# Nine up-projection pairs of a float32 encoder layer by seven half-size products

## The chip, the core and the metric

One core of a Trainium2 chip runs the whole layer in one launch. The metric is the device time of one execution in microseconds (us). The engines are named as the profile names them: PE (TensorE, matrix products), PEld (its weight loads), DVE (VectorE), ACT (ScalarE), POOL (GpSimd), SP (SyncE, which only issues DMAs here). SBUF is the on-chip memory of 128 partitions; PSUM holds the sums that PE writes, in banks of 128x512 float32. [...] A change of 0.2% of the time, 2.1 us, is about what a measurement of this kernel can tell from no change.

## What is computed

The last sub-layer, the gated MLP, is what the change touches (512 tokens, 1024 channels, 2816 hidden channels):

```python
hf = _rms_norm(x, norm_ffn_pre[l])
u = _dwconv_causal(hf @ w_up[l], ffn_dw[l]) + ffn_dw_b[l]
u_g, u_v = jnp.split(u, 2, axis=-1)
yff = (jax.nn.silu(u_g) * u_v) @ w_down[l]
x = x + _rms_norm(yff, norm_ffn_post[l])
```

`w_up` holds the 2816 gate columns and then the 2816 value columns. The convolution has width 3 and runs along the tokens.

## The kernel before

Every float32 product is made of three: an operand is split into a rounded high part and the rest, and `mm3` (lines 253 to 257 before the change) issues high x high, high x low and low x high. A weight block comes from HBM into a raw tile; ACT casts it to the high part `wh` (line 201) and DVE subtracts to get the low part `wl` (line 202). `run_blocks` walks a list of jobs (a load, then a body of products) and prepares three jobs ahead; four `wh`/`wl` tiles go round, so a cast waits until PE is done with the block four splits earlier. A scheduler then sets the order of the instructions on each engine when the program is built; each engine works its list in that order, and an instruction that waits holds back all that stands behind it.

**Up projection** (`up_jobs`). The 22 gate/value pairs j are blocks of 128 columns: one gate job and one value job each, of 24 products of 128x512 (8 channel tiles, three products each), the activations `hth`/`htl` as the moving operand. The first four jobs (j = 0, 1) run in two token halves, as 128x256 products, since the second half of the tokens is normalized last. `done` evacuates a bank: ACT applies the last tap and the bias (line 1639), DVE adds the two other taps (line 624), and after the value block ACT takes silu and DVE multiplies into a quarter tile `qa`/`qb` (line 1645).

**Down projection.** It already uses Strassen's seven products over pairs of hidden tiles and column and token halves. Its weight sums are made during the up projection by `Sums`: two rows of blocks of `w_down` come in over ACT's DMA queue into `dw` tiles (line 568), four sums are made in place by DVE (lines 572 to 575), and the result is stored to DRAM over ACT's queue (line 579) and read back later by SP. Its activation sums are made by GpSimd from the quarter tiles (`activation_sums`, lines 596 to 599), four operations of 128x256 a pair. There are four `dw` tiles, and two row pairs are in flight.

Of the kernel before, what the change touches and what calls it, by code (L numbers as in the profile page):

```python
# [17 lines left out]
F32 = mybir.dt.float32  # L18
F32R = mybir.dt.float32r
AF = mybir.ActivationFunctionType  # L20
ALU = mybir.AluOpType
# [4 lines left out]
P = 128  # L26
# [60 lines left out]
def hybrid_layer(ctx: ExitStack, tc: tile.TileContext, a: dict, out: bass.AP):  # L87
# [120 lines left out]
    def cols(w, c0, n=P, k0=0, nk=NK):  # L208

        return w[k0 * P:(k0 + nk) * P, c0:c0 + n].rearrange("(k p) c -> p k c", p=P), [P, nk, n]  # L210
# [29 lines left out]
            body(*w)  # L240
            bg.tick()

    def matmul(ps, lhs, rhs, start, stop):
        steps_of[:] = [PE.matmul(ps, lhs, rhs, start=start, stop=stop).ins]  # L244
        bg.clock += max(int(math.prod(rhs.shape[1:])), 256) * 0.00042

    turns = []
# [2 lines left out]
        turns.append(PE.transpose(ps, x, ident[:n, :n]).ins)  # L250
        bg.clock += 0.107

    def mm3(ps, w_hi, w_lo, x_hi, x_lo, first, last):

        matmul(ps, w_hi, x_hi, first, False)
        matmul(ps, w_hi, x_lo, False, False)
        matmul(ps, w_lo, x_hi, False, last)

    def channel_major(ps, w, act, sl=slice(0, S), turn=None):

# [296 lines left out]
    class Sums:  # L557
# [9 lines left out]
                for i, x in enumerate(self.held[q]):  # L567
                    self.queue.dma_start(x, self.w[(2 * q + i) * P:(2 * q + i + 1) * P, :])

        def add(self, q):  # L570
            (b11, b12), (b21, b22) = ((x[:, :S], x[:, S:]) for x in self.held[q])
            V.tensor_tensor(b22, b22, b12, ALU.subtract)
            V.tensor_tensor(b12, b12, b11, ALU.subtract)
            V.tensor_tensor(b11, b22, b11, ALU.add)
            V.tensor_tensor(b21, b21, b11, ALU.subtract)

        def store(self, q):
            for i, x in enumerate(self.held.pop(q)):
# [15 lines left out]
    def activation_sums(x, z, eng):  # L594

        eng.tensor_tensor(x[:, 2], x[:, 1], z[:, 1], ALU.add)
        eng.tensor_tensor(x[:, 3], x[:, 0], x[:, 1], ALU.subtract)
        eng.tensor_tensor(x[:, 1], x[:, 2], x[:, 0], ALU.subtract)
        eng.tensor_tensor(z[:, 2], z[:, 0], x[:, 1], ALU.subtract)
# [597 lines left out]
    def then(f):  # L1197

        return None, None, f
# [420 lines left out]
    def open_ffn():  # L1620
        bg.drain("n1")
        close(ns.work_)
        close(ns.xp_)
        close(ns.xm_)
        ns.fp_, ns.fp = new_pool("ffn", False)
        ns.work = ns.fp
        ns.quart = [(ns.fp.tile([P, 4, S // 2], F32, tag=f"qa{q}", name="qa"),
                     ns.fp.tile([P, 3, S // 2], F32, tag=f"qb{q}", name="qb")) for q in range(NF // 2)]
        ns.post = ns.fp.tile([P, D], F32, name="g_ffn")
        G.dma_start(ns.post, a["norm_ffn_post"][0].partition_broadcast(P))  # L1630

    def up_jobs():
        st, held = {}, []

        def done(j, i, ps):
            if i == 0:
                st[j] = ns.fp.tile([P, 2, S], F32, tag="c", name="c", bufs=2)
            c, ch = st[j], i * NF + j
            st["first"] = A.activation(c[:, i], ps, AF.Identity, bias=pc("fb", ch), scale=pc("fdw2", ch)).ins
            st["taps"] = taps(c[:, i], ps, lambda k: pc("fdw01", k * 44 + ch), 3).ins  # L1640
            if i == 1:
                th = ns.fp.tile([P, S], F32, tag="th", name="th")
                A.activation(th, c[:, 0], AF.Silu)  # L1643
                x = ns.quart[j // 2]
                V.tensor_tensor(x[j % 2][:, 0:2].rearrange("p a b -> p (a b)"), th, c[:, 1], ALU.mult)
                if j % 2:
                    activation_sums(*x, G)


        for n in range(2 * NF):  # L1650
            def body(hi, lo, n=n):
                j, i = divmod(n, 2)
                if n > 3:
                    ps = bank()
                    channel_major(ps, (hi, lo), ns.hf)
                    done(j, i, ps)

                    q = n // 3 - 2
                    if 0 <= q < NF // 2:
                        with tc.issue_after(st["taps" if n % 3 == 0 else "first"]):  # L1660
                            (ns.sums.add, ns.sums.store, ns.sums.load)[n % 3](q + 2 * (n % 3 == 2))
                    return
                if n == 0:
                    bg.drain("n0")
                ps = bank(("mm", "sc")[n % 2])
                if n == 3:
                    channel_major(ps, (hi, lo), ns.hf, slice(0, S // 2), lambda: bg.drain("n1"))
                else:
                    (channel_major if n else by_pass)(ps, (hi, lo), ns.hf, slice(0, S // 2))
                held.append((j, i, ps, (hi, lo)))  # L1670
                if n == 3:
                    open_ffn()
                    for j, i, ps, w in held:
                        (channel_major if i or j else by_pass)(ps, w, ns.hf, slice(S // 2, S))
                        done(j, i, ps)
# [3 lines left out]
                    ns.sums.load(1)  # L1679
            yield *cols(w_up, n % 2 * DFF + n // 2 * P), body, V, same, HALF_SHIFT if n < 4 else 0  # L1680

    def down_jobs():
        pairs, hold, half = NF // 2, 4, S
# [7 lines left out]
                load_parts(raw, ns.sums.parts(phase, job, q))  # L1691
                raws.append(raw)

        def split_to(hi, lo, x):
            A.copy(hi, x)  # L1695
            V.tensor_tensor(lo, x, hi.bitcast(F32), ALU.subtract)  # L1696

        def activations(phase, q):

            if (phase, q) == (0, 0):  # L1700
                hi, lo = (gp.tile([P, WB], F32R, tag="wr", name="wr", bufs=2) for _ in range(2))
            elif (phase, q) == (1, pairs - 1):
                hi, lo = (ns.fp.tile([P, D], F32R, tag=f"qa{i}", name="a3") for i in range(2))
            else:
                if "slots" not in parts:
                    parts["slots"] = [t[:, i * 4:i * 4 + 4].rearrange("p a b -> p (a b)") for t in new_ht()
                                      for i in range(2)]
                slot = parts["slots"][(phase * pairs + q - 1) % 4]
# [3 lines left out]
            split_to(hi, lo, ns.quart[q][phase].rearrange("p a b -> p (a b)"))  # L1712
# [22 lines left out]

        def step(name, t, q, a, w, phase, cut=slice(0, S), ps=None):
            hi, lo = parts[phase, q]
            sl = slice(t * P, (t + 1) * P)
# [166 lines left out]
```

## Time and profile before

| | |
|---|---|
| time, median of 3 runs | 1040.89 us (1040.86 to 1042.05) |
| span of the profiled execution | 1039.2 us; its own time is not given apart from the span |
| PE busy | 1029.6 us, 99% |
| DVE / ACT / POOL busy | 819.5 / 510.9 / 153.2 us |
| up projection from the third pair on | from about 709 to 932 us of the span |
| down projection | from there to the end |

A row of a group reads: line, engine, operation, output and inputs, shape, count, then total busy time and mean of one, then the idle time of the engine ahead of it and what ended it. A row of one source line gives least, median and greatest duration in ns. A matmul's own duration overlaps its neighbours', so the pace of PE is read from the distance of starts.

### The profile page before, as it was taken

How to read it: one execution, taken by the hardware profiler on the slowest of the kernel's cores; microseconds unless marked ns; L12 is line 12 of the kernel's file. 1: busy time of each engine (PE TensorE's matmuls, PEld its weight loads, DVE VectorE, ACT ScalarE, POOL GpSimd, SP SyncE). 2: the span in 40 equal slices, each digit the busy share in tenths (PEclk: the TensorE clock that was granted, in tenths of full speed). 3: DMA queues.
4: the chain of work that ended last, by engine and by line, in shares of the span. 5: the costliest groups of instructions: out<-in, count | busy, mean ns of one | idle time of the engine just before them, and what ended most of it. 6: DMA issues, size and time to landing. Idle time of an engine off the chain costs nothing.

```text
span 1039.2 us, 14390 instructions
## 1 busy us (share of the span) xinstructions
PE 1029.6 (99%) x5189; PEld 876.3 (84%) x5189; DVE 819.5 (79%) x1263; ACT 510.9 (49%) x838; POOL 153.2 (15%) x235
## 2 busy tenths in 40 slices
PE   9999999999999999999999999999999999999997
PEld 8888888888888988888888899898888888888886
DVE  7999999577788668878687898767777767667796
ACT  5322222376565465765634566645333433445672
POOL 4001000100020214342000021121112121111002
PEclk9999999999999999999999999999999999999999
DMA  8954333334534345766467744145677676625662
GB/s 272 320 155 97 102 102 102 83 100 114 150 99 131 88 131 167 203 172 168 143 199 251 239 137 123 46 138 166 199 239 235 211 236 207 213 82 191 216 212 82
DMA packets 194125, 169.36 MB, mean 163 GB/s; under 512 B 25295, under 2 KB 165692, under 8 KB 194053
## 3 DMA queue, kind: packets, MB, share of 16 engines
q1 hardware_dynamic: 185011, 136.69, 43.9%
q10 hardware_dynamic: 6482, 23.21, 6.1%
q0 software_dynamic: 2560, 8.54, 2.8%
q8 instruction: 41, 0.67, 0.3%
q14 instruction: 31, 0.25, 0.1%
HBM read 142.18 MB, written 26.23 MB: 162 GB/s over the span
## 4 chain that ended last, share of the span: by engine, by line
PE 96%; DMA 2%; DVE 1%; ACT 0%; issue 0%; SPq 0%; POOL 0%; POOLq 0%; DVEq 0%; ACTq 0%
PE ps_mm L244 46%; PE ps_av L244 30%; PE ps_tr L244 11%; PE ps_sc L244 7%; PE ps_tr L250 1%; DMA turned<-e 1%; DMA ptl<-turned 1%; PE ps_mm L462 1%; PE ps_av L462 1%; DMA xs<-in_x 0%; DVE e L857 0%; DVE e L939 0%; DVE e L930 0%; PE ps_tr L446 0%; DVE wl L202 0%
## 5 line engine op out<-in xcount | busy, mean ns | idle before, releaser
L201 ACT CAST wh<-wr 128x1024 fp32r<-128x1024 f32 (+1 forms) x140 | 146.3, 1047 | 235.3 <-PE ps_mm L244 119.3
L202 DVE TENSOR_TENSOR wl<-wr,wh 128x1024 fp32r<-128x1024 f32 (+1 forms) x140 | 175.1, 1251 | 83.1 <-ACT wh L201 81.2
L244 PE MATMUL ps_mm<-hth,wh 128*128 128x512 f32 (+1 forms) x536 | 198.3, 377 | 0.0
L244 PE MATMUL ps_mm<-htl,wh 128*128 128x512 f32 (+1 forms) x536 | 198.3, 377 | 0.0
L244 PE MATMUL ps_mm<-hth,wl 128*128 128x512 f32 (+1 forms) x536 | 198.1, 377 | 0.0
L244 PE MATMUL ps_av<-htl,wh 128*128 128x512 f32 (+1 forms) x328 | 122.5, 373 | 0.0
L244 PE MATMUL ps_av<-hth,wh 128*128 128x512 f32 (+1 forms) x328 | 122.4, 373 | 0.0
L244 PE MATMUL ps_av<-hth,wl 128*128 128x512 f32 (+1 forms) x328 | 122.3, 373 | 0.0
L244 PEld LDWEIGHTS ps_mm<-hth,wh 128*128 128x128 f32 x536 | 99.1, 188 | 18.3 <-ACT hth L164 0.3
L244 PEld LDWEIGHTS ps_mm<-hth,wl 128*128 128x128 f32 x536 | 98.9, 188 | 18.2
L244 PEld LDWEIGHTS ps_mm<-htl,wh 128*128 128x128 f32 x536 | 99.0, 188 | 18.0
L697 DVE SCALAR_TENSOR_TENSOR y<-y,par,y 128x508 f32<-128x508 f32 (+29 forms) x120 | 82.8, 731 | 0.1
L244 PEld LDWEIGHTS ps_av<-hth,wl 128*128 128x128 f32 x328 | 61.7, 188 | 11.0
L244 PEld LDWEIGHTS ps_av<-htl,wh 128*128 128x128 f32 x328 | 61.5, 188 | 10.9
L244 PEld LDWEIGHTS ps_av<-hth,wh 128*128 128x128 f32 x328 | 61.6, 188 | 10.8
L1696 DVE TENSOR_TENSOR wl<-dw,wh 128x1024 fp32r<-128x1024 f32 x32 | 40.2, 1261 | 16.8 <-ACT wh L1695 16.6
L1695 ACT CAST wh<-dw 128x1024 fp32r<-128x1024 f32 x32 | 33.5, 1052 | 24.5 <-PE ps_tr L244 10.1
L1643 ACT ACTIVATE th<-c 128x512 f32<-128x512 f32 x22 | 13.9, 632 | 48.6 <-DVE c L624 48.6
L624 DVE SCALAR_TENSOR_TENSOR c<-ps_mm,par,c 128x510 f32<-128x510 f32 (+1 forms) x44 | 32.7, 744 | 0.7
L857 DVE STREAM_TRANSPOSE e<-e 128x128 f32<-128x128 f32 (+3 forms) x46 | 32.5, 729 | 0.2
L876 DVE TENSOR_TENSOR ptl<-ptl,pth 128x384 fp32r<-128x384 f32 (+3 forms) x42 | 20.7, 511 | 14.9 <-ACT pth L875 14.8
L244 PE MATMUL ps_tr<-htl,wh 128*128 128x512 f32 x80 | 31.7, 396 | 0.0
(518 smaller groups left out, 2238.5 us busy)
## 6 DMA issues: line engine op xcount, KB each, us to landing
wr<-in_w_up SPq DMA_DIRECT2D x44, 512.0 KB
wr<-in_w_in SPq DMA_DIRECT2D x38, 512.0 KB
wr<-in_w_gate SPq DMA_DIRECT2D x32, 512.0 KB
wp<-in_w_down ACTq DMA_DIRECT2D x22, 512.0 KB
sums<-wp ACTq DMA_DIRECT2D x22, 512.0 KB
dw<-sums SPq DMA_DIRECT2D x44, 256.0 KB
wr<-in_w_branch SPq DMA_DIRECT2D x16, 512.0 KB
wide<-in_w_out SPq DMA_DIRECT2D x12, 512.0 KB
```

Source lines behind the costliest of these rows:

```text
L201: last_weights[:] = [order(A.copy(hi, raw[:, :n])).ins, low.tensor_tensor(lo, raw[:, :n], hi.bitcast(F32), ALU.subtract).ins]
L202: low.tensor_tensor(lo, raw[:, :n], hi.bitcast(F32), ALU.subtract).ins]
L244: steps_of[:] = [PE.matmul(ps, lhs, rhs, start=start, stop=stop).ins]
L250: turns.append(PE.transpose(ps, x, ident[:n, :n]).ins)
L462: keep(PE.matmul(banks[c][:, :S // 2], w[p == 1][:, k, c * P:(c + 1) * P], ht[p == 2][:, i * 4 + k, :S // 2], start=(i, p, k) == (0, 0, 0) ...
L624: ins = V.scalar_tensor_tensor(dst[:, s:], src[:, :S - s], w(k), dst[:, s:], ALU.mult, ALU.add)
L697: ins = V.scalar_tensor_tensor(dst[:, s:], src[:, :S - s], pc("conv_dw", k * 4 + j), dst[:, s:], ALU.mult, ALU.add)
L857: V.transpose(dst, src.rearrange("p (t j b) -> p b t j", b=4, j=32))
L876: V.tensor_tensor(lo, raw, hi.bitcast(F32), ALU.subtract)
L1643: A.activation(th, c[:, 0], AF.Silu)
L1695: A.copy(hi, x)
L1696: V.tensor_tensor(lo, x, hi.bitcast(F32), ALU.subtract)
```

## The change

Pairs j = 3, 5, ... 19 get the seven products; each is followed by an ordinary pair j+1, and I call the two a group, 1 to 9. Pairs 0, 1, 2 and 21 stay ordinary. For a seven-product pair the two blocks are cut in halves by channels (a11, a12 the gate block, a21, a22 the value block), and the activations in halves by channels and tokens. Each product then has 4 channel tiles, three products each, of 128x256: 7 x 12 = 84 products of 128x256 where there were 48 of 128x512.

- `token_sums`: once, GpSimd makes four sums of activations (eight operations of 128x1024, lines 1639 and 1641), and ACT and DVE split them into `tokh`/`tokl` (lines 1646, 1647).
- For each seven-product pair both blocks come into two `dw` tiles (named `wq`, line 1740), and GpSimd makes four sums of 128x512 in place and in `sums2` (lines 1732 to 1735). Four splits follow: the gate block (for step a), s2 and s1 (step b), the changed value block (step c) and half of the gate tile (step d, 128x512). The products run as a (24), b (24), c (12), d (12) and e (12, with the weights of c).
- Banks: the results gather in one `sc` and one `tr` bank; three 128x256 copies by ACT (lines 1757, 1763, 1765) and three 128x256 additions by DVE in PSUM (lines 1759, 1770, 1774) stand between the products.
- The `w_down` row sums of pairs 1 to 10 go from DVE to GpSimd (`add`, four operations of 128x512 a group); pair 0 stays on DVE. One pair is loaded ahead, not two.
- The value block of the ordinary pair is cut in two halves of 12 products around c and d.
- The activation sums of the down projection are three operations (lines 1658 to 1660), made from the last group on, and a fourth (line 1862) after the split of phase 0; the split of a pair in phase 0 is two of 128x512, not one of 128x1024.

```diff
-        def add(self, q):
+        def add(self, q, eng=V):
...
-            V.tensor_tensor(b22, b22, b12, ALU.subtract)
+            eng.tensor_tensor(b22, b22, b12, ALU.subtract)
...
+    def token_sums():
...
+        for i, (k, t) in enumerate(((0, 0), (1, 1), (0, 1), (1, 0))):
+            x = [h.bitcast(F32)[:, 4 * k:4 * k + 4, cut[t]] for h in ns.hf]
+            G.tensor_tensor(raw[i], *x, ALU.add)
+        for out, a, b in ((0, 2, 0), (2, 1, 2), (1, 1, 0), (3, 3, 1)):
+            G.tensor_tensor(raw[out], raw[a], raw[b], ALU.subtract)
+        for i in (1, 0, 2, 3):
+            split_to(hi[:, i], lo[:, i], raw[i])
...
+    def down_sums(*pairs):
+
+        for q in pairs:
+            x, t = ns.quart[q], ns.pair_sums[q]
+            G.tensor_tensor(t[:, 0], x[:, 1], x[:, 3], ALU.add)
+            G.tensor_tensor(t[:, 1], x[:, 0], x[:, 1], ALU.subtract)
+            G.tensor_tensor(x[:, 1], t[:, 0], x[:, 0], ALU.subtract)
...
+            def load_a():
+                z.g, z.v = [load_block(j, i) for i in range(2)]
+                w = split_weights(z.g, [P, NK, P], shift=HALF_SHIFT)
+                z.s = ns.fp.tile([P, D], F32, tag="z7", name="sums2")
...
+                G.tensor_tensor(s1, a21, a22, ALU.add)
+                G.tensor_tensor(s2, s1, a11, ALU.subtract)
+                G.tensor_tensor(a21, a11, a21, ALU.subtract)
+                G.tensor_tensor(a12, a12, s2, ALU.subtract)
...
+            def load_block(j, i):
+                raw = ns.fp.tile([P, D], F32, tag="dw", name="wq", bufs=4)
...
+            yield a
+            yield then(lambda q=q: ns.sums.load(q + 1))
+            yield plain(j + 1, 0)
+            yield b
+            yield then(lambda q=q: ns.sums.add(q + 1, G))
+            yield (*block(j + 1, 1), first_half)
...
+            yield c
+            yield d
+            yield then(lambda q=q: ns.sums.store(q + 1))
+            yield then(lambda j=j, f=second_half: f(j + 1))
+            yield e
```

**GpSimd's list**, in the middle of the up projection. Before, the activation sums of two pairs (`qa`, `qb` are quarter tiles):

```order
L597 TENSOR_TENSOR qa_6866<-qa_6866 128x256 [waits DVE_49]
L596 TENSOR_TENSOR qa_6866<-qa_6866,qb_6867 128x256 [waits DVE_49]
L598 TENSOR_TENSOR qa_6866<-qa_6866 128x256 [waits Pool_49]
L599 TENSOR_TENSOR qb_6867<-qb_6867,qa_6866 128x256 [waits Pool_49]
L597 TENSOR_TENSOR qa_6868<-qa_6868 128x256 [waits DVE_49]
```

Now, one whole group, the sixth (`wq_8041` and `wq_8043` are its gate and value blocks, `wp_8180` and `wp_8181` two rows of `w_down`):

```order
L1732 TENSOR_TENSOR sums2_8049<-wq_8043 128x512 [waits DMAHW2_49,DVE_49]
L1733 TENSOR_TENSOR sums2_8049<-sums2_8049,wq_8041 128x512 [waits DMAHW1_49,Pool_49]
L1734 TENSOR_TENSOR wq_8043<-wq_8041,wq_8043 128x512 [waits DMAHW6_49]
L572 TENSOR_TENSOR wp_8181<-wp_8181,wp_8180 128x512 [waits DMAHW4_49,DMAHW3_49,DVE_49]
L1735 TENSOR_TENSOR wq_8041<-wq_8041,sums2_8049 128x512 [waits DMAHW5_49,DVE_49,Pool_49]
L573 TENSOR_TENSOR wp_8180<-wp_8180 128x512 [waits Pool_49]
L574 TENSOR_TENSOR wp_8180<-wp_8181,wp_8180 128x512 [waits Pool_49]
L575 TENSOR_TENSOR wp_8181<-wp_8181,wp_8180 128x512 [waits Pool_49]
L1732 TENSOR_TENSOR sums2_8259<-wq_8253 128x512 [waits DMAHW2_49,DVE_49]
```

Eight operations of 128x512 stand in one row of work where four of 128x256 stood for each pair, and the first waits for the DMA of the value block.

**ACT's list**, at a store of `w_down` sums. Before, with DVE making the sums:

```order
L1639 ACTIVATE c_7360<-ps_av_7374,par2_406 128x512 [waits PE_49]
L579 DMA sums_7004<-wp_7202 128x1024 [waits DVE_49]
L579 DMA sums_7004<-wp_7203 128x1024 [waits DVE_49]
L201 CAST wh_7448<-wr_7446 128x1024 [waits DMAHW3_49,PE_49]
L1639 ACTIVATE c_7438<-ps_mm_7413,par2_406 128x512 [waits PE_49]
```

Now, at the same stores of the sixth group (`wh_8086` is the high part for its step b, `wh_8184` for its step c):

```order
L579 DMA sums_6869<-wp_8180 128x1024 [waits DMAHW6_49,DMAHW3_49,Pool_49]
L1671 ACTIVATE c_8103<-ps_sc_7941,par2_406 128x512 [waits DVE_49]
L1757 COPY mu_8153<-ps_tr1_8152 128x256 [waits PE_49,Activation_49]
L579 DMA sums_6869<-wp_8181 128x1024 [waits DMAHW4_49,Pool_49]
L201 CAST wh_8086<-sums2_8049 128x1024 [waits PE_49]
L1671 ACTIVATE c_8103<-ps_tr0_7942,par2_406 128x512 [waits PE_49]
L201 CAST wh_8184<-wq_8043 128x1024 [waits DMAHW2_49,PE_49]
L1675 ACTIVATE th_8142<-c_8103 128x512 [waits DVE_49,Activation_49]
```

The store of the second row waits for GpSimd's last operation of the group, and the cast for step b stands behind it.

**SP's list** of block loads at the same place. Before, each load waits for a raw tile that DVE has read:

```order
L185 DMA wr_7690<-in_w_up 128x8x128 [waits DMAHW4_49,DVE_49]
L185 DMA wr_7731<-in_w_up 128x8x128 [waits DMAHW0_49,DVE_49]
L185 DMA wr_7768<-in_w_up 128x8x128 [waits DMAHW7_49,DMAHW1_49,DVE_49]
L185 DMA wr_7813<-in_w_up 128x8x128 [waits DMAHW4_49,DVE_49]
L185 DMA wr_7852<-in_w_up 128x8x128 [waits DMAHW7_49,DMAHW2_49,DVE_49]
```

Now (`wr` are blocks of the ordinary pair, `wq` those of the seven-product pair):

```order
L185 DMA wr_8067<-in_w_up 128x8x128 [waits DMAHW7_49,DVE_49]
L185 DMA wr_8145<-in_w_up 128x8x128 [waits DMAHW5_49,DMAHW0_49,DVE_49]
L1740 DMA wq_8041<-in_w_up 128x8x128 [waits DMAHW4_49,DMAHW3_49,DMAHW5_49,DMAHW1_49,Pool_49]
L1740 DMA wq_8043<-in_w_up 128x8x128 [waits DMAHW6_49,DMAHW4_49,DMAHW2_49]
L185 DMA wr_8277<-in_w_up 128x8x128 [waits DMAHW7_49,DVE_49]
```

The four `dw` tiles now serve both the blocks and the `w_down` rows, and a new tile takes the buffer that the scheduler expects to be free first. In the built program the blocks of groups 6 to 9 take the two buffers of the `w_down` rows of the group before (`wq_8041` that of `wp_7970`, `wq_8043` that of `wp_7971`), so their loads wait for those stores; the `w_down` rows in turn take the buffers of the blocks, after the splits for c and d. Group 3 takes those of group 2's blocks; groups 4 and 5 take one of each kind.

More of the change, by code (lines that the diff above doesn't have):

```diff
@@ L241, in run_blocks, with matmul @@
             bg.tick()
[L243 to L244 removed]
+    def matmul(ps, lhs, rhs, start, stop, again=False):
+        steps_of[:] = [PE.matmul(ps, lhs, rhs, start=start, stop=stop, skip_group_check=again).ins]
         bg.clock += max(int(math.prod(rhs.shape[1:])), 256) * 0.00042
@@ L1643, in done, with block, add_sums, sums_step @@
                 A.activation(th, c[:, 0], AF.Silu)
[L1644 to L1650, printed above, removed]
+                x = ns.quart[j // 2][:, 2 * (j % 2):2 * (j % 2) + 2]
+                V.tensor_tensor(x.rearrange("p a b -> p (a b)"), th, c[:, 1], ALU.mult)
+        def block(j, i):
+            return cols(w_up, i * DFF + j * P)
+        def add_sums(q, eng, anchor):
+            with tc.issue_after(st[anchor]):
+                ns.sums.add(q, eng)
+        def sums_step(what, q, anchor):
+            if q < NF // 2:
+                with tc.issue_after(st[anchor]):
+                    getattr(ns.sums, what)(q)
+        def plain(j, i, then=None):
+            def body(hi, lo):
+                ps = bank()
+                channel_major(ps, (hi, lo), ns.hf)
+                done(j, i, ps)
+                if then:
+                    then()
+            return *block(j, i), body
+        for n in range(4):
             def body(hi, lo, n=n):
                 j, i = divmod(n, 2)
[L1653 to L1662, printed above, removed]
                 if n == 0:
@@ L1682, in down_jobs @@
+        q = NF // 2 - 1
+        yield then(lambda: (ns.sums.load(q), down_places(("tokh", 8), ("tokl", 1))))
+        yield plain(NF - 1, 0, lambda: (ns.sums.add(q, G), down_sums(2, 3)))
+        yield plain(NF - 1, 1, lambda: (ns.sums.store(q), down_sums(*range(4, NF // 2))))
     def down_jobs():
```

121 lines of the change are left out of this document (101 added, 20 removed).

## The prediction

> **What bounds the kernel now.** I read the page's busy times first, then the chain that ended last, then the stretch of the up projection from its third pair on.
>
> ```profile
> span 1039.2 us, 14390 instructions
> PE 1029.6 (99%) x5189; PEld 876.3 (84%) x5189; DVE 819.5 (79%) x1263; ACT 510.9 (49%) x838; POOL 153.2 (15%) x235
> PE 96%; DMA 2%; DVE 1%; ACT 0%; issue 0%; SPq 0%; POOL 0%; POOLq 0%; DVEq 0%; ACTq 0%
> 709.40:931.80 222.40, 222.40 (x983) 184.06 (x982) 160.40 (x192) 88.85 (x110) 36.40 (x41) 1.00 0.61 199
> ```
>
> PE is the bound: 96% of the chain, and in the last row (windows: length, then busy time of PE, PEld, DVE, ACT, POOL, the granted clock, the DMA share) it is busy for all 222.4 us at full clock. DVE is at 72%, GpSimd at 16%. Fewer or cheaper products are time won only while the others keep up. The span lies 1.7 us under the median of 1040.9; I add the sum to the median.
>
> **PE.** One piece of the chain is a block of 24 products of 128x512; two starts, with 33 others between them, give the pace of 128x256:
>
> ```profile
> 747.68 5.44 PE ps_av L244 x24
> ...
> 704.93 0.28 PE L244 MATMUL ps_mm<-hth,wh 128*128 128x256 f32 x1
> ...
> 708.94 0.28 PE L244 MATMUL ps_sc<-hth,wl 128*128 128x256 f32 x1
> ```
>
> So 5.44 / 24 = 0.2267 us, and 4.01 / 34 = 0.1179 us: a half-width product costs 52%. Nine pairs lose 48 x 0.2267 = 10.88 and gain 84 x 0.1179 = 9.90: **-0.98 a pair, -8.9 in all**. The built lists have 432 products of 128x512 fewer and 756 of 128x256 more, as said. A group takes PE 9.90 + 10.88 = 20.78.
>
> **What the group now asks of DVE, ACT and GpSimd.** Prices:
>
> ```profile
> L201 ACT CAST wh<-wr 128x1024 fp32r<-128x1024 f32 x38 | 39.8, 1048 | 75.4 <-PE ps_mm L244 60.4 <-PE ps_av L244 10.0 <-DMA wr<-in_w_up 4.9
> L202 DVE TENSOR_TENSOR wl<-wr,wh x38: 1210/1226/1756, 710.6 to 906.3; 128x1024 fp32r<-128x1024 f32 x38
> L1645 DVE TENSOR_TENSOR qa<-th,c x11: 682/692/693, 709.7 to 919.9; 128x512 f32<-128x512 f32 x11
> L624 DVE SCALAR_TENSOR_TENSOR c<-ps_mm,par,c x44: 734/744/751, 704.3 to 924.6; 128x510 f32<-128x510 f32 x22, 128x511 f32<-128x511 f32 x22
> L435 POOL TENSOR_TENSOR wa<-e,wa x4: 1276/1304/1307, 7.9 to 12.6; 128x512 fp32r<-128x512 f32 x4
> L597 POOL TENSOR_TENSOR qa<-qa x11: 731/739/1122, 710.5 to 920.7; 128x256 f32<-128x256 f32 x11
> ```
>
> DVE per group: five splits of 1.23 and one of about 0.69 (the multiply of 128x512 as its price), two multiplies of 0.69, eight tap additions of 0.744, and three PSUM additions of 128x256. The trace has none of those; they lie between nothing and the 0.69 of a 128x512 operation, I take 0.42. Sum 15.5 of 20.78: DVE alone is hidden. The three copies and one and a half casts more on ACT (88.85 of 222.4 busy) hide in its idle time. GpSimd: eight operations of 1.30, 10.4 per group, where it had 8 x 0.74 = 5.9.
>
> But GpSimd and DVE do not run beside each other freely:
>
> ```profile
> 780.28 1.11 DVE L574 TENSOR_TENSOR wp<-wp 128x512 f32<-128x512 f32 x1
> 780.93 1.07 POOL L598 TENSOR_TENSOR qa<-qa 128x256 f32<-128x256 f32 x1
> 781.32 1.76 DVE L202 TENSOR_TENSOR wl<-wr,wh 128x1024 fp32r<-128x1024 f32 x1
> 782.07 1.60 POOL L599 TENSOR_TENSOR qb<-qb,qa 128x256 f32<-128x256 f32 x1
> 783.00 1.22 DVE L575 TENSOR_TENSOR wp<-wp 128x512 f32<-128x512 f32 x1
> ```
>
> Five operations whose prices alone are 0.69, 0.74, 1.23, 0.74 and 0.69 lengthen each other in turn: each waits until the one on the other engine is over. Line 624, which reads PSUM and one SBUF tile, never took over 0.751. So only DVE operations on two SBUF tiles are shut out.
>
> **The loop that sets the pace.** From group 6 on, by the lists shown, this goes round once a group: GpSimd's last row sum (575) releases the store of that `w_down` row on ACT; its buffer is the next value block's; SP loads the block; GpSimd makes all eight sums; the next 575. Behind the store on ACT stands the cast for step b, and PE's list waits at b. Prices of the two transfers:
>
> ```profile
> 750.52 0.33 ACTq L579 DMA_DIRECT2D sums<-wp  x1
> ...
> 755.86 0.34 ACTq L568 DMA_DIRECT2D wp<-in_w_down  x1
> 712.31 0.37 SPq L185 DMA_DIRECT2D wr<-in_w_up  x1
> 716.26 1.05 ACT L201 CAST wh<-wr 128x1024 fp32r<-128x1024 f32 x1 [3.55 <-DMA wr<-in_w_up]
> xin<-in_x POOLq DMA_DIRECT2D x4, 512.0 KB, 4.4
> ```
>
> A second store behind a first let its buffer be refilled after 5.3 us. A load was waited for 3.95 us after its issue; the page gives another of 512 KB 4.4. For a store with less beside it I take 4.5 (between the 3.95 of the shortest transfer and 5.3), for the load 4.4. GpSimd's eight take 1.304 each and 0.08 between dependent ones:
>
> ```profile
> 715.61 0.74 POOL L596 TENSOR_TENSOR qa<-qa,qb 128x256 f32<-128x256 f32 x1 [4.41 <-DVE qb L1645]
> 716.43 0.75 POOL L598 TENSOR_TENSOR qa<-qa 128x256 f32<-128x256 f32 x1
> ```
>
> (0.82 from start to start), so 8 x 1.384 = 11.0. Loop: 4.5 + 4.4 + 11.0 = **19.9 without shutting out**, under the 20.78 of PE. While GpSimd's eight run, DVE has the splits for a, for both ordinary blocks and one multiply to do: 3 x 1.23 + 0.69 = 4.4, which lengthens the eight by 0 to 4.4. The five operations above lost about all their overlap; an operation at the edges of the eight costs nothing, so I take 3.2. Loop 23.1, 2.3 over PE's 20.78. It binds between 575 of group 5 and 575 of group 9, four times: **+9.2**, between 0 (loop of 20.8 or less) and 14 (24.3).
>
> A second way round is about as long: 575, cast and split for b, evacuations, split for c, then for d, which releases a buffer for the next `w_down` row (some 10 us on ACT and DVE by the prices above), load 4.4, GpSimd's last five 6.9: 21.3. It does not go below the first once shutting out is added.
>
> **Entering it.** In group 5 the loads come from buffers released by the split for d of group 4. PE's list before b is e (1.41), a (2.83), the ordinary block (5.44) and nine products of the next (2.04): b is due 11.7 into the group, and the block ends there too. Split for d: 11.7 + 0.6 + 0.7 + some latency = 13.2; load to 17.6; eight sums 11.0 and 3.2: 31.8, that is 11.0 into group 5. Store issue, cast and split for b, 0.33 + 1.05 + 1.23 = 2.6: 13.6 against 11.7, **+2**, between 0 and 3.2.
>
> **The start.** GpSimd's token sums begin when the last `htl` is there:
>
> ```profile
> 697.78 1.29 DVE L165 TENSOR_TENSOR htl<-ps_tr,hth 128x512 fp32r<-128x512 f32 x2 [2.31 <-ACT hth L164]
> ```
>
> at 699.1. A sum of 128x1024 does not stand in the trace; by the two sizes of GpSimd above it is 1.30 + 2 x 0.565 = 2.43. By the built list seven of these and three block sums come ahead of what b needs: 20.9, at 720.0; cast and split, 722.3. PE is at b at 709.4 + 2 x 5.44 + 2.83 + 5.44 = 728.6. The cover is 6.3 us; against it, ten operations, each held up to 0.6 (half a split), and DVE now has four token splits of 1.23 and its own row sums in the same 30 us. In group 2 the cast for a stands behind the store that waits for GpSimd. I take **+2.5**, between 0 and 6.
>
> **The down projection.** 9 x 3 pair sums of 0.74, eleven of line 1862 and four of 1.30, 33 us, now fall into the stretch after the last group, where DVE's splits are all of two SBUF tiles: about 3.8 us for each pair's 24 products of 5.44. In turn with four GpSimd operations a pair that is 3.8 + 3.0 = 6.8, so DVE falls 1.3 behind per pair, for some six or seven pairs, 8 to 9 us; three blocks prepared ahead cover 3 x 2.72 = 8.2 less cast and split. **+2**, between 0 and 5.
>
> **Sum:** -8.9 + 9.2 + 2 + 2.5 + 2 = +6.8: 1047.7, I say **1048**.
>
> [...]
>
> **The rivals.**
> - *PE stays the bound.* If store, load and shutting out stay under 9.8 together (4.0 + 3.95 + 1.8, say), the loop hides, the entry and the down projection cost nothing, and what is left is -8.9 + 2.5: 1034.5, at best 1032. For it: DVE and GpSimd have idle time left even in sum (15.5 and 10.4 of 20.78), and an operation held back need not be one that is waited for. Against it: the loop's fixed part is 19.9 already. It decides at a loop of 20.8.
> - *The loop binds a little,* at 21.3: 4 x 0.5 + 0.5 + 2.5 + 2 - 8.9 = -1.9, about 1039 to 1043 with its bounds.
> - *Every DVE operation in the eight is paid in full:* loop 24.3, +14, entry 3.2, start 2.5, down 5: +15.8, 1057. For it: the five rows. [...]
> - That fewer products are saved than said is excluded by the lists.
>
> **How the numbers follow.** Loop of about 23 (1043 to 1053): 0.40. Full price: 0.18. A little (1038.8 to 1043): 0.12. PE the bound: 0.30. A change under 0.2%, 2.1 us, can't be told from none, so faster 0.30, same 0.12, slower 0.58. The range runs from the middle of the PE-bound case to the full price, 1033 to 1057; what lies outside is about 0.06 below and 0.09 above.
>
> **What would show it.** Right: PE idle at the first `tokh` products of groups 5 to 9, 2 us each, released by ACT or DVE on `sums2`; ACT idle ahead of it until POOL line 575; GpSimd's operations of 128x512 at 1.6 to 1.8 in the mean, not 1.3; groups 20.8 apart in the middle and about 23 at the end; DVE's line 202 well above its median of 1.226. Wrong: PE busy throughout and groups 20.8 apart (first rival); or the idle time elsewhere, as at step a or d behind a block's DMA, or at the down projection's splits. The forecast falls with the store and load: at 3 us each the loop is 20.2.

## The result and the profile after

The changed kernel takes **1073.6 us** in the median of four runs (1072.0 to 1075.1), against 1040.9 for the kernel before on the same chip: a ratio of **1.0309, 95% interval 1.0294 to 1.0324**. Slower was forecast, but +7 us and at most +16; it is +33.

The page of the changed kernel: span, busy times, and the chain that ended last by engine.

```profile
span 1070.5 us, 15271 instructions
PE 1034.7 (97%) x5513; PEld 889.1 (83%) x5513; DVE 858.4 (80%) x1283; ACT 536.9 (50%) x898; POOL 308.6 (29%) x319
PE 75%; POOL 12%; DMA 7%; issue 2%; DVE 2%; ACT 1%; ACTq 0%; POOLq 0%; SPq 0%; DVEq 0%
```

PE's share of the chain falls from 96% to 75%; GpSimd and DMA, which had 0 and 2%, now carry 19%, though GpSimd is busy for only 29% of the span. It is waited for in places, not on the whole. The stretches show which. First the kernel before (up projection from 709.4 on, down projection), then the changed one, cut at step b of group 2 and at the first product of the down projection (length, busy PE, PEld, DVE, ACT, POOL, granted clock, DMA share):

```profile
709.40:927.00 217.60, 217.60 (x962) 180.20 (x961) 156.70 (x188) 84.06 (x104) 36.40 (x41) 1.00 0.62 201
927.00:1039.20 112.20, 105.26 (x475) 87.32 (x474) 86.53 (x97) 62.53 (x83) 8.51 (x16) 0.98 0.50 167
```

```profile
709.40:760.00 50.60, 45.69 (x245) 39.28 (x244) 42.80 (x45) 22.90 (x30) 26.68 (x15) 0.97 0.48 157
760.00:945.50 185.50, 172.56 (x1045) 153.54 (x1044) 137.47 (x156) 84.15 (x122) 114.89 (x75) 0.97 0.56 182
945.50:1070.50 125.00, 109.21 (x475) 87.84 (x474) 102.31 (x110) 66.19 (x96) 45.07 (x47) 0.97 0.50 170
```

The up projection took 217.6 us and takes 236.1, the down projection 112.2 and 125.0. PE has idle time in all three stretches, and its granted clock is under 1 in each. I put a number on this with the two paces of the prediction: for each product the distance to the next start, less 0.2267 us (128x512) or 0.1179 us (128x256), summed over a stage. I call the sum the stage's **loss**: **start** (709 to step b of group 2) 7.6 us, **middle** (to the end of the up projection) 19.4, **down** 13.0. In the kernel before they are 0.0, 0.0 and 0.2. The account closes: 1039.2 - 8.9 + 40.0 = 1070.3, against a span of 1070.5. Of the 40.0, about 7 is lost at a granted clock of 0.50 (last section); the rest is idle.

**Middle.** The loop that was foreseen stands in the chain piece by piece, here from 575 of group 5 to 575 of group 6 (start, length, what):

```profile
828.87 2.65 DMA sums<-wp
...
831.60 4.97 DMA wq<-in_w_up
...
836.70 1.51 POOL sums L1732
...
838.28 1.30 POOL sums L1733
839.58 2.13 POOL wq L1734
...
841.84 2.21 POOL wp L572
844.04 1.25 POOL wq L1735
845.30 2.24 POOL wp L573
...
847.61 1.63 POOL wp L574
...
850.63 2.70 DMA sums<-wp
```

Store 2.65, load 4.97, eight sums 13.9: 21.8 us round, where PE needs 20.8. GpSimd's sums take 1.25 to 1.3 with no split beside them and about 2.2 when a DVE split, of 1.23 by itself, runs beside them. I call the distance from one group's 575 to the next group's a **turn**; from group 3 to group 9 it is 21.95 us in the mean. One of the four turns that I priced, from group 7 to group 8, does not follow this loop in the chain: there the chain goes through PE, DVE's split for d and the load of a `w_down` row, the second way round of the prediction:

```profile
875.32 5.43 PE ps_mm L244 x21
...
882.11 1.79 DVE wl L202
883.91 3.35 DMA wp<-in_w_down
```

And PE feels the loop elsewhere than I wrote. ACT in group 3:

```profile
785.61 2.03 ACTq L579 DMA_DIRECT2D sums<-wp  x2
787.68 0.62 ACT L201 CAST wh<-wq 128x512 fp32r<-128x512 f32 x1 [6.61 <-POOL wp L575]
...
791.26 0.82 ACTq L568 DMA_DIRECT2D wp<-in_w_down  x2
792.12 0.37 ACT L1763 COPY mu<-ps_tr 128x256 f32<-128x256 f32 x1 [3.14 <-DMA sums<-wp]
```

ACT stands 6.6 us at the stores, then 3.1 more at the next rows' loads, which wait until a store has left its buffer. Behind both stands the copy that step c needs: PE idles from 788.1 to 792.5. In group 7 an evacuation stands 7.2 us behind a store that waits for 574, and behind it stands a cast of the ordinary block, for which PE waits 4.0 us:

```profile
870.47 0.78 ACT L1671 ACTIVATE c<-ps_sc,par 128x512 f32<-128x512 f32 x1 [7.16 <-POOL wp L574]
871.14 1.03 ACT L201 CAST wh<-wr 128x1024 fp32r<-128x1024 f32 x1
...
PE ps_mm L244 <- ACT wh L201: 4.0, 1, 4.0
```

(the last row is of waits: us in total, times, longest). At step b of groups 5 to 9, where I looked for 2 us each, PE waits once, 1.1 us in group 6.

**Start.** DVE's splits while GpSimd makes token sums of 128x1024:

```profile
703.50 2.85 DVE L202 TENSOR_TENSOR wl<-wr,wh 128x1024 fp32r<-128x1024 f32 x1 [4.09 <-ACT wh L201]
...
706.93 2.77 DVE L202 TENSOR_TENSOR wl<-wr,wh 128x1024 fp32r<-128x1024 f32 x1
...
710.94 3.33 DVE L202 TENSOR_TENSOR wl<-wq,wh 128x1024 fp32r<-128x1024 f32 x1
...
717.15 3.41 DVE L202 TENSOR_TENSOR wl<-wr,wh 128x1024 fp32r<-128x1024 f32 x1
...
721.80 3.38 DVE L1647 TENSOR_TENSOR tokl<-qa,tokh 128x1024 fp32r<-128x1024 f32 x1
```

Alone each takes 1.23 (the median of 1.226 before): these five lose 9.6 us, and DVE is busy for 31.5 of the 31.6 us up to 741. Step b of group 1, due at 729.5, starts at 731.9.

**Down.** GpSimd's pair sums and DVE's splits in turn, both lengthened, and ACT behind the row sums of pair 10:

```profile
952.45 1.18 POOL L1660 TENSOR_TENSOR qa<-pairs,qa 128x256 f32<-128x256 f32 x1
952.96 1.22 DVE L1647 TENSOR_TENSOR hth<-qa,hth 128x512 fp32r<-128x512 f32 x1
953.59 1.18 POOL L1862 TENSOR_TENSOR qa<-qa 128x256 f32<-128x256 f32 x1
...
954.11 1.22 DVE L1647 TENSOR_TENSOR hth<-pairs,hth 128x512 fp32r<-128x512 f32 x1
...
964.64 1.71 POOL L573 TENSOR_TENSOR wp<-wp 128x512 f32<-128x512 f32 x1
...
972.63 1.28 POOL L574 TENSOR_TENSOR wp<-wp 128x512 f32<-128x512 f32 x1
...
974.38 1.04 ACT L1646 CAST wh<-dw 128x1024 fp32r<-128x1024 f32 x1 [8.49 <-POOL wp L574]
```

A split of 128x512 takes 1.22 where 0.69 is its time alone (684 ns least in e8, below), a pair sum 1.18 where it is 0.74 (line 597 before). The chain runs through GpSimd's list alone from 939.9 to 976.5, without a pause:

```profile
939.87 1.72 POOL pairs L1658
...
952.49 1.15 POOL qa L1660
...
975.28 1.25 POOL wp L575
```

L572 to L575 of pair 10 stand between pair sums of all pairs; until the store behind 575 lands, at 980.7, they hold two of the four `dw` buffers through which the down projection's blocks come. PE's longest wait there, 3.75 us up to 967.5, is for the split of such a block, whose cast waited for its load:

```profile
964.32 1.04 ACT L1646 CAST wh<-dw 128x1024 fp32r<-128x1024 f32 x1 [2.75 <-DMA dw<-sums]
```

### The profile page after: what moved, and what is told of

It reads as the page before. It is cut to its first block, busy times and chain, and to the rows that moved or that the text cites. A ratio compares the mean times of both kernels' runs of the same rounds, so it can differ in the third digit from the quotient of the medians.

```text
span 1070.5 us, 15271 instructions
## 1 busy us (share of the span) xinstructions
PE 1034.7 (97%) x5513; PEld 889.1 (83%) x5513; DVE 858.4 (80%) x1283; ACT 536.9 (50%) x898; POOL 308.6 (29%) x319
## 4 chain that ended last, share of the span: by engine, by line
PE 75%; POOL 12%; DMA 7%; issue 2%; DVE 2%; ACT 1%; ACTq 0%; POOLq 0%; SPq 0%; DVEq 0%
PE ps_mm L244 36%; PE ps_av L244 19%; PE ps_tr L244 10%; PE ps_sc L244 7%; DMA wq<-in_w_up 3%; POOL wp L573 2%; DMA sums<-wp 2%; POOL wp L572 2%; POOL wp L574 2%; DMA wp<-in_w_down 1%; PE ps_tr L250 1%; POOL wq L1735 1%; POOL sums L1732 1%; POOL qa L1660 1%; DVE wl L202 1%
## 5 line engine op out<-in xcount | busy, mean ns | idle before, releaser
L244 PE MATMUL ps_mm<-hth,wh 128*128 128x512 f32 (+1 forms) x464 | 170.8, 376 | 4.4 <-ACT wh L201 4.0
L244 PE MATMUL ps_mm<-htl,wh 128*128 128x512 f32 (+1 forms) x464 | 170.7, 376 | 0.0
L244 PE MATMUL ps_mm<-hth,wl 128*128 128x512 f32 (+1 forms) x464 | 170.4, 376 | 0.0
L244 PE MATMUL ps_av<-htl,wh 128*128 128x512 f32 (+1 forms) x256 | 95.1, 371 | 0.0
L244 PE MATMUL ps_av<-hth,wh 128*128 128x512 f32 (+1 forms) x256 | 95.0, 371 | 0.0
L202 DVE TENSOR_TENSOR wl<-wq,wh 128x1024 fp32r<-128x1024 f32 (+1 forms) x27 | 34.3, 1270 | 17.2 <-ACT wh L201 14.8
L244 PE MATMUL ps_tr<-hth,wh 128*128 128x512 f32 (+1 forms) x116 | 41.9, 362 | 2.5 <-ACT wh L201 2.5
L244 PE MATMUL ps_tr<-htl,wh 128*128 128x512 f32 (+1 forms) x116 | 41.7, 360 | 0.0
L244 PE MATMUL ps_tr<-hth,wl 128*128 128x512 f32 (+1 forms) x116 | 41.5, 358 | 0.0
L244 PE MATMUL ps_tr<-tokh,wh 128*128 128x256 f32 x108 | 31.6, 292 | 9.5 <-ACT mu L1763 6.1
```

The costliest lines, as they stand in the source:

```text
L202: low.tensor_tensor(lo, raw[:, :n], hi.bitcast(F32), ALU.subtract).ins]
```

## The experiments

Theory: the loop through the shared buffers makes the middle's loss, the token sums the start's, and the pair sums with pair 10's row sums the down projection's. Rivals: ACT's stands at the stores alone; GpSimd and DVE taking the same time from each other whoever does the sums; PE not saving the 8.9. Every kernel gets a new order on all engines when it is built, so a stage that an edit does not touch can still differ by some us (down is 11 to 20 in kernels that leave it as it was). The ratio is to the kernel before on the same chip; the turn is the mean of the six from group 3 to group 9. It is the pace that came out, so a wait of any cause lengthens it.

| kernel | median us | ratio, 95% interval | start | middle | down | turn |
|---|---|---|---|---|---|---|
| as changed | 1073.6 | 1.0309 (1.0294 to 1.0324) | 7.6 | 19.4 | 13.0 | 21.95 |
| e1_rows_dve | 1067.4 | 1.0250 (1.0234 to 1.0265) | 8.1 | 15.2 | 11.4 | 20.6 |
| e2_stores_pool | 1078.6 | 1.0356 (1.0339 to 1.0373) | 6.0 | 23.5 | 15.4 | 23.95 |
| e4_down_dve | 1072.9 | 1.0298 (1.0266 to 1.0330) | 7.5 | 22.5 | 14.3 | 22.3 |
| e5_blocks_dve | 1071.6 | 1.0298 (1.0272 to 1.0324) | 4.4 | 19.4 | 20.1 | 22.0 |
| e3_own_places | 1067.4 | 1.0246 (1.0226 to 1.0266) | 10.0 | 8.4 | 17.3 | (cut) |
| e7_no_rows | 1044.0 | 1.0027 (1.0016 to 1.0037) | 5.1 | -0.4 | 6.6 | |
| e8_no_pair_sums | 1062.0 | 1.0199 (1.0183 to 1.0214) | 7.3 | 19.3 | 1.6 | 22.1 |
| e9_no_rows_no_pair_sums | 1037.8 | 0.9966 (0.9956 to 0.9976) | 7.9 | -0.4 | 2.0 | |
| e10_rows_moved_only | 1053.8 | 1.0120 (1.0104 to 1.0135) | 13.7 | 0.1 | 7.5 | |
| e11_no_token_sums | 1034.8 | 0.9929 (0.9913 to 0.9946) | 0.1 | -0.3 | 2.4 | |
| e12_own_places_rows_dve | 1062.5 | 1.0202 (1.0187 to 1.0217) | 9.1 | 8.8 | 12.1 | (cut) |
| e13_rows_not_stored | 1067.0 | 1.0245 (1.0228 to 1.0262) | 7.5 | 8.7 | 18.0 | 20.8 |

In each row 1039.2 - 8.9 + the three losses gives the span of the profiled execution within 1.5 us. The losses are those of that execution; in e4 and e5 it is 3.7 and 5.1 us longer than the median beside it.

**e1_rows_dve.** `ns.sums.add(q + 1, G)` becomes `ns.sums.add(q + 1)`, and so does the last `add`.

> The w_down row sums of pairs 1 to 10 go back to DVE; the seven-product pairs, their block sums and the pair sums stay as changed. Of the changed kernel's 32.7 us over the kernel before, its trace puts 7.6 us of PE idle or slowed time ahead of step b of group 2, 19.4 from there to the end of the up projection, 13.0 into the down projection, against 8.9 saved. Theory A (GpSimd's train of eight stands in front of everything: the store, the next load, and ACT's casts behind the store): with four operations gone from it the 19.4 falls to 5 or less, and ACT's stand of 8.5 us in the down projection goes, worth 3 to 6 there: 1048 to 1056. Theory B (GpSimd and DVE shutting each other out is the loss, whoever does the sums): DVE gets 2.8 us a group more and GpSimd 5.2 less, the sum of both falls by a quarter of what they share, and the 19.4 falls by a quarter: about 1065 to 1069. Theory C (the loads of the blocks behind the shared buffers are the loss, not the sums): no change within 3 us.

1067.4, with 15.2 left in the middle: both as B said. That does not show B's reason. The turn is 20.6 in the mean, but 22.0 to 22.4 from group 6 to group 9, and a new wait stands at the head of DVE's list:

```profile
DVE wp L572 <- DMA wp<-in_w_down: 11.7, 6, 3.2
```

DVE, with splits and evacuations behind it, stands for the rows' loads, which wait for the shared buffers. Pair 10's row sums are on DVE too, and down is still 11.4.

**e2_stores_pool.** `(G if self.queue is A else self.queue).dma_start(...)` in `store`.

> The stores of the w_down row sums are issued by GpSimd behind its own sums, so that ACT no longer stands at them; buffers, loads and all sums stay. Theory A1 (ACT standing at the stores, 22.1 + 13.3 us in the trace, holds the copies and casts that PE waits for): most of the 19.4 us between step b of group 2 and the end of the up projection goes, since what PE needs of GpSimd are the first two of its eight sums, and the 8.5 us stand in the down projection too: 1052 to 1060. Theory A2 (the way round through store, buffer and load sets the pace, ACT's list does not matter): the way round is as long as before and two DMA issues longer on GpSimd: 1073 to 1080.

1078.6, as A2 said: the turn grows to 23.95 and the middle with it. It does not clear ACT altogether, since the rows' loads stay in its list and still wait for the stores (27.8 us in the middle); so e2 alone does not exclude A1.

**e4_down_dve.** `G.` becomes `V.` in lines 1658 to 1660 and 1862.

> The activation sums of the down projection (three per pair and the fourth behind the split) are made by DVE, not GpSimd; the up projection up to the last group stays. Theory D1 (the 13.0 us lost in the down projection are GpSimd's 44 operations of 128x256, at 1.1 to 1.7 us each where I had 0.74, with pair 10's row sums and ACT's store behind them): on DVE an operation takes some 0.42 us, and DVE's splits of 128x512 fall from 1.22 to 0.69: the loss falls to 0 to 4, 1061 to 1065. Theory D2 (DVE is the bound there, 43.5 of 49 us busy): DVE gets 44 x 0.42 = 18.5 us more work ahead of and in the down projection, and the loss stays or grows: 1073 to 1080.

1072.9, no gain: D2, 0.1 below its range. DVE's price was as estimated, 0.42 us (median of line 1659: 422 ns), and it is full, busy for 26.87 of 27.00 us:

```profile
948.00:975.00 27.00, 20.74 (x69) 14.67 (x68) 26.87 (x46) 12.29 (x19) 2.90 (x3) 0.81 0.48 161
```

One operation of GpSimd, met by ten such DVE sums and a split in a row, took 6.31 us for its 1.28:

```profile
940.44 6.31 POOL L572 TENSOR_TENSOR wp<-wp 128x512 f32<-128x512 f32 x1 [18.91 <-DMA wp<-in_w_down]
```

**e5_blocks_dve.** `G.` becomes `V.` in lines 1732 to 1735.

> The four block sums of each seven-product pair are made by DVE, the w_down row sums stay on GpSimd: GpSimd and DVE get the same work as where the row sums go to DVE and the block sums stay, but ACT's store still waits for GpSimd, and the down projection is as changed. Theory A (length of the train): the way round is store 3 to 4.5, load 5, DVE's four at 0.7, GpSimd's four at 1.3 to 2.2, some 18 us against PE's 20.8: the 19.4 falls to 5 or less, 1056 to 1060. Theory B (shutting out, whoever does which): as the other exchange in the up projection, 1066 to 1070. Theory E (who waits for whom: DVE's list is held up where a block sum waits for its DMA, and the evacuations and splits stand behind it): over 1073.

1071.6: neither A nor B, and just under E's mark. In its long execution the middle is 19.4 and the turn 22.0; what E named is there, DVE's list standing for the blocks:

```profile
DVE sums L1732 <- DMA wq<-in_w_up: 11.1, 5, 5.3
```

**e3_own_places.** The blocks of groups 2 to 6 leave the shared buffers:

```diff
-                raw = ns.fp.tile([P, D], F32, tag="dw", name="wq", bufs=4)
+                g = (j - 1) // 2
+                if 2 <= g <= 6:
+                    raw = ns.quart[(7 if g % 2 else 9) + i].rearrange("p a b -> p (a b)")
+                else:
+                    raw = ns.fp.tile([P, D], F32, tag="dw", name="wq", bufs=4)
```

> The gate and value blocks of the seven-product pairs of groups 2 to 6 come into quarter tiles that are not yet written at that time, two pairs of them in turn, so that no block of these groups shares a buffer with a w_down row; all sums, stores and their engines stay. The changed kernel loses 19.4 us between step b of group 2 and the end of the up projection, some 16 of it up to group 7. Theory S (the way round through the shared buffers sets the pace: store, refill, sums, next store; who makes the sums matters little, as moving four of them to DVE gained only 6 us): about two thirds of the 19.4 go, 1058 to 1064. Theory A1 (ACT stands at stores that wait for GpSimd, whatever the buffers): 1070 to 1075. Theory O (the lists' orders are built on durations that GpSimd and DVE do not keep once they shut each other out, so waits of 1 to 4 us turn up wherever two engines hand over): 1068 to 1075, with the waits at other places.

The middle falls by 11.0 of 19.4, a little less than the two thirds that S said, with every sum, store and engine as before; A1 had no such fall. What is left is mostly one wait at c of group 2 (3.2 us; the granted clock is 0.98 in the mean from 761.0 to 936.7). The time is 3 us above S's range since start and down came out 6.7 worse.

**e7_no_rows, e8_no_pair_sums, e9.** e7 drops `load`, `add` and `store` of pairs 1 to 10, and `parts` hands out rows of `w_down`; e8 makes `down_sums` empty, drops line 1862 and splits `x[:, 2:]` in place of the pair sums; e9 is both.

> Left out: the w_down row sums of pairs 1 to 10, with their loads and stores; the down projection reads the rows of w_down themselves in their place. GpSimd has four operations a group, no store stands in ACT's list, and the four buffers hold blocks alone. Theory S and theory A1: the 19.4 us go but for 0 to 4, and the stand of 8.5 us in the down projection goes: 1045 to 1054. Theory O or a loss that sits in the seven products' own hand-overs (casts, splits, copies, block sums): at least half of the 19.4 stays: 1060 or more.

> Left out: the activation sums of the down projection (three operations per pair and the fourth behind the split); the splits read other parts of the same quarter tiles in their place. The up projection up to the last group stays. Theory D1 (GpSimd's 44 operations in the stretch are the loss of 13.0, by their time and by shutting DVE out; on DVE they cost it about as much, which is why the move to DVE gained nothing): the loss falls to 0 to 4: 1062 to 1066. Theory D3 (pair 10's row sums and the store on ACT, or the splits being two of 128x512, are the loss): 8 or more stay: 1069 or more.

> Both left out: the row sums of pairs 1 to 10 (the rows are read in their place) and the activation sums of the down projection. What is left is the saving in products with the token sums and the block sums alone. If the products save 8.9 as counted and the start costs the 7.6 that the changed kernel's trace shows: 1041 - 8.9 + 7.6 + 0 to 4 = 1040 to 1044. If the block sums and the splits of the seven products alone hold PE up: 1048 or more.

These settle most. e7, at 1044.0, is 1 us below its range. Without the rows PE has no gap from b of group 2 to the end of the up projection:

```profile
756.10:923.00 166.90, 166.90 (x1051) 150.81 (x1050) 124.70 (x156) 86.32 (x123) 59.33 (x41) 1.00 0.35 102
```

So in the middle the seven products' own casts, splits, copies and block sums cost nothing by themselves; the 19.4 comes with the rows. Down falls to 6.6 without the rows, to 1.6 without the pair sums, whose absence also shows the splits alone (least, median, greatest in ns):

```profile
L1647 DVE TENSOR_TENSOR hth<-qa,hth x16: 684/692/959, 952.7 to 1024.2; 128x512 fp32r<-128x512 f32 x12, 128x768 fp32r<-128x768 f32 x4
```

D1 holds, and D3 falls: without the pair sums, pair 10's rows cost next to nothing. With the pair sums they count: down is 6.6 and 7.5 in the two kernels that keep the pair sums and have no row sums of pair 10 (e7, e10), and 11 or more in all that have both. e9 comes out below its range, at 1037.8. Its profiled execution is the longest of its runs (1041.6), so its losses, of which the start has 7.9, are probably higher than usual.

**e10_rows_moved_only.** Only the two `add` calls of pairs 1 to 10 are dropped.

> Left out: only the four operations on each w_down row pair from 1 to 10; the rows are still loaded into the shared buffers and stored from them, unchanged, over ACT's queue. So far: without rows altogether the 19.4 us of the up projection between step b of group 2 and its end went to nothing (and the down projection's 13.0 to 6.6); with the row sums on DVE 15.2 stayed; with blocks of groups 2 to 6 in places of their own 8.4 stayed. Theory S (the way round through four shared buffers, whoever sums): loads and stores are all still there, GpSimd's train is 5 to 9 us shorter a group: 8 to 15 of the 19.4 stay, 1060 to 1068. Theory A (GpSimd's train of eight is the long leg of the way round): at most 4 of the 19.4 stay, and the down projection is at about 6.6: 1046 to 1054.

Middle 0.1: A, not S. The loads and stores with four sums a group fit; with eight the loop is too long. The time is 1053.8, at the top of A's range, because a of group 2 waited 6.4 us for its block in this order (start 13.7).

**e11_no_token_sums.** e9, and in `token_sums` the eight `G.tensor_tensor` go; `raw[i] = x[0]`.

> Left out: the row sums of pairs 1 to 10, the activation sums of the down projection, and the eight token sums of 128x1024 by GpSimd as well (the splits read parts of the high activations in their place). Beside the kernel that leaves out the first two only (1037.8), this prices the start, 7.9 us there. Theory T1 (GpSimd's operations of 2.4 us shut out DVE, whose splits of 128x1024 beside them took 2.8 to 3.4 us where one alone takes 1.23, and DVE's list runs late): the 7.9 falls to 0 to 2.5: 1030 to 1033. Theory T2 (DVE has four more splits of 1.23, row sums and evacuations in 30 us, and is full whatever GpSimd does): 4 or more stay: 1034 to 1038.

```profile
709.40:751.80 42.40, 42.40 (x246) 37.43 (x245) 34.24 (x45) 20.46 (x28) 12.82 (x8) 1.00 0.53 162
```

The start's loss is gone, as T1 said, and PE has no gap where T2 kept 4 us or more. But the median drops by 3.0 only: it lies in T2's range, 1.8 above T1's, probably because e9's usual start is cheaper than the one in its profile. Whether the splits held up by GpSimd (9.6 us above) or the late token sums weigh more stays open: here the token splits also come earlier.

**e12_own_places_rows_dve.** The edits of e3 and e1 together.

> Nothing left out: the blocks of groups 2 to 6 in quarter tiles that are not yet written, and the row sums on DVE. With own places and row sums on GpSimd 8.4 of the 19.4 us stayed, and 1067.4 in all, since the down projection and the start lost 27.3 together. Theory S: with places of their own the engine of the row sums is free to choose, DVE's are shorter, ACT's stands too: the middle loses 2 to 6, the rest about as in the changed kernel (7.6 + 13.0) or 3 us less without pair 10's row sums on GpSimd: 1052 to 1060. Theory A1 (ACT's stands are what is left there): the same, with the middle at 0 to 2. If it is above 1063, the row sums on DVE cost DVE what they spare GpSimd.

1062.5, 2.5 above S's range, and the best that computes the layer. The middle is 8.8 where S had 2 to 6 and A1 0 to 2, no better than with own places alone. PE's waits there have moved, from ACT's copies (4.2 us in e3) to DVE's additions in PSUM:

```profile
PE ps_tr L244 <- DVE ps_tr L1774: 4.8, 3, 3.1
```

So with the loop cut, moving the row sums to DVE gains nothing there.

**e13_rows_not_stored.** The `store` calls go, and `parts` hands out rows as in e7.

> Left out: the stores of the row sums of pairs 1 to 10 (the down projection reads the rows of w_down in their place). The rows are loaded and all sums are made by GpSimd as in the changed kernel, in the shared buffers. Theory L (the way round 575, store, load, eight sums, 575, in the changed kernel 21.9 us a group from group 3 on, against 20.8 for PE): it loses one leg of 2.65 us, 19.3 are left, so the loop no longer binds: of the 19.4 us at most 6 stay, and the first three groups hold them: 1050 to 1060, the down projection at 8 to 13. Theory B (the time of GpSimd's eight sums and what they take from DVE, wherever they wait): all of that work is still there, 14 or more of the 19.4 stay: 1063 to 1072.

All of GpSimd's work is there, one leg of 2.65 us is not: the turn is 20.8, PE's own, and the middle falls by 10.7. That is nearer L, though 8.7 is above the 6 it allowed; B, which kept 14 or more, falls. The time is in B's range only because the down projection is at 18.0 (its order changed too). Without stores ACT does not stand at them either, so e13 does not part the leg from ACT's stands.

No kernel here that computes the layer beats the one before. With all three kinds of extra sums left out the time is 1034.8, 7 us below before; with the row sums alone free (e7) the time is still 0.27% above it. To win the 7 us, the cost of the rows, of the pair sums and of the token sums would all have to go.

## Why the prediction was wrong, point by point

- **PE, -8.9:** right. Where nothing holds PE up, in the middle of e7, e9 and e11, it keeps the two paces within 0.4 us.
- **GpSimd's price:** right. 1.28 us alone; 1.65 in the mean of the 68 operations from 740 to 925, with DVE's splits beside some of them, in the 1.6 to 1.8 forecast. DVE's splits pay too: 18 of 41 were lengthened, and the mean of all is 1.53. The median stays at 1.226, so "well above its median" was the wrong sign to look for.
- **The loop:** right as a mechanism, shown by e10, e13 and e3, which take out sums, a leg and the sharing. The turn from group 5 to 9 is 22.5 us against 23.1: store 2.8 for 4.5, load 5.7 for 4.4, sums 13.8 for 14.2. (22.5 - 20.78) x 4 = 7 of the 9.2. Two things in it were wrong: one of the four turns went the second way round, which I had put below the first, and PE waited at step b only once; that the size came out near is in part luck.
- **Entering it, +2:** too small, and late by two groups. From b of group 2 (760.0) to b of group 5 (832.0) PE lost 72.0 - 3 x 20.78 = 9.6. I let the loop bind from 575 of group 5 on, and ahead of that I followed only the cast for b of group 5. But in the chain a store of group 3 (785.6) already releases a block load (790.1), and in groups 2 and 3 ACT's stands at stores and row loads already hold back the copy that c needs (line 1763), one of the three that I said would hide in ACT's idle time.
- **The start, +2.5:** 7.6. I held GpSimd's ten operations up by half a split each; I named DVE's added splits, but counted no lengthening of DVE's own operations, which lost 9.6 on five.
- **The down projection, +2: the step that failed most,** 13.0. I let DVE, in turn with GpSimd, fall 1.3 behind per pair, and let three blocks prepared ahead cover 8.2 of it. The price in turn was not too low: a pair sum and a split together take 1.14 us from start to start (952.45 to 953.59), less than the 0.74 + 0.69 that I took. The cover failed. GpSimd's list ran without a pause to 976.5, 31 us into the stage, with the first two sums of seven pairs in front of the third of any of them; and pair 10's row sums, last due, stood among them with two of four buffers and ACT's store behind them. That was to be read from the built list of GpSimd, of which I priced the sum and not the order. How the 13.0 divides is open: without the pair sums 1.6 is left (e8), without the rows 6.6 (e7), but with pair 10's row sums only moved to DVE still 11.4 (e1).
- **No term at all:** the granted clock of 0.50 behind four gaps, about 7 us.
- **Rivals.** "PE stays the bound" (1034.5) is e11's time, which needs all three sums gone. "Paid in full" (1057) had the sign and the places, and was 17 short. The three kernels that move sums back to DVE (e1, e4, e5) gained 6, 1 and 2 us.

Down +11.0, middle +8.2 and start +5.1 above their terms make 24.3 (the time at a clock of 0.50 within them). Between the medians the miss is 25.9; the profiled execution is 1.3 us shorter than the median of the changed kernel.

## What to carry to other kernels

A buffer shared by two streams ties their engines, queues and transfers into one loop; write down its legs, and ask at which instruction *any* list stands in it, for the loss appears behind that one. Where an engine's new work is put in at a stage's seam, read the order in which it stands there: the work due last may stand in front, holding buffers. And a wait that PE feels can cost more than its length: here about 7 us at a granted clock of 0.50 came on top of PE's idle time.

## What the runs showed of the hardware

**The granted clock changed at multiples of 3.41 us.** In the trace of the changed kernel it is 0.50 from 733.13 to 736.54, 791.15 to 797.98, 873.07 to 876.48 and 968.64 to 972.06, and from 1067.63 on, and 1.00 in between. From the first of these changes to the last the stretches are 3.41, 54.61, 6.83, 75.09, 3.41, 92.16, 3.41 and 95.57 us long: 1, 16, 2, 22, 1, 27, 1 and 28 times 3.413. Around the gap at 868 to 872 (the row as above; PE busy is the second number, the clock the third from the end):

```profile
866.25:869.66 3.41, 1.94 (x17) 1.74 (x15) 0.00 (x0) 0.00 (x0) 3.35 (x3) 1.00 0.51 150
869.66:873.08 3.42, 0.85 (x4) 0.72 (x5) 1.62 (x2) 2.61 (x4) 1.66 (x2) 1.00 0.62 255
873.08:876.49 3.41, 3.41 (x10) 2.65 (x9) 3.41 (x6) 2.60 (x4) 0.00 (x0) 0.50 0.85 253
876.49:879.90 3.41, 3.41 (x17) 2.78 (x16) 3.41 (x6) 0.00 (x0) 0.00 (x0) 1.00 0.93 273
```

PE idled 1.5 us of the first stretch and the next was at 1.00; it idled 2.6 of the second and the third was at 0.50. In that trace, cut at the same multiples from 700 us to the last product, four stretches at 1.00 hold 2.2 to 2.9 us of PE idle (from 729.72, 787.74, 869.66 and 965.24), and each is followed by one at 0.50. The other stretches at 1.00 hold 1.6 or less, and each is followed by one at 1.00. The gap from 788.1 to 792.5 was followed by two at 0.50 (to 797.98). PE was busy for 15.7 us at a clock of 0.50 before the last product; half of that, 7.8, bounds what it cost, and the distances of starts put it at about 7.

**Plain sums of GpSimd and DVE lengthened each other.** In e4 one operation of GpSimd, met by DVE's sums and a split in a row, took 6.31 us for its 1.28. They did not exclude each other in full: one of each took 1.14 us in turn (952.45 to 953.59, start to start) where the two alone take 0.74 and 0.69. Line 624, with one input in PSUM, was not lengthened: in the changed kernel 51 of its 88 operations from 706 us on ran beside one of GpSimd and took 0.731 to 0.750 us, the other 37 0.733 to 0.752.
